# Feed-forward tile sums and splits moved from GpSimd to VectorE, with separated rings, four banks for the first pair and a pool shared by both products

## The chip, the cores and the metric

The kernel runs on one core of one Trainium2 chip. The metric is the device time of one execution in microseconds (us). Engines are named as in the profile: PE (TensorE, matmuls), DVE (VectorE), ACT (ScalarE), POOL (GpSimd), and SP, whose queue issues the DMAs.

## The reference

One decoder layer on a sequence of 1024 tokens of width 1024: an input projection, a state-space group and a sparse-attention group side by side, an output projection, and then the feed-forward part. The change touches the end of the output projection and the feed-forward part:

```
    mixed = jnp.concatenate([rms_norm(y_ssm, gn_ssm[i]), rms_norm(y_att, gn_attn[i])], axis=-1)
    x = x + g1 * (mixed @ w_out[i])
    h2 = rms_norm(x, norm2_g[i]) * (1.0 + sc2) + sh2
    ff = jnp.square(jax.nn.relu(h2 @ w_ff1[i])) @ w_ff2[i]
    x = x + g2 * ff
```

`w_ff1` is 1024 x 4096, `w_ff2` 4096 x 1024, all float32.

## The kernel before

Every float32 operand of a matmul is split in two float32r tiles: `hi`, a rounded copy made on ACT, and `lo`, the rest `x - hi`, a subtraction on DVE or POOL (`split`). A product of two such pairs is three matmuls, hi·hi, hi·lo and lo·hi (`mm3`, lines 89 to 91).

Both feed-forward products use a Strassen-Winograd scheme: 7 half-size products in place of 8, for which tiles must be added and subtracted first (operand sums) and results added and subtracted afterwards.

**Output projection (`outproj`).** Eight sequence tiles t = 0..7. `proj(t)` multiplies, and its result (`xn`, `x1`) is normalised; `modulate(t)` transposes it, scales it (`h`) and splits it into B: `b00`, `b10` for tiles 0 to 3, `b01` (called T1) and `b11` for tiles 4 to 7. T1 and `b11` are whole only after `modulate(7)`.

**First product (`ff_up`).** 16 steps i, each 256 columns of `w_ff1` (tile `w1r`, a ring of 2 buffers). Steps 0 and 1 are `plain` (8 products of 12 matmuls, no Winograd). Steps 2 to 15 are 7 products each: `prep` makes weight forms (`wsum` on POOL into ring `ws`, then `split` into ring `wf`), `step` multiplies. `tform(2..4)` make three more right-hand operands `t2`, `t3`, `t4` from the h tiles, by POOL subtractions (lines 1618 to 1622) and splits. `put` evacuates a bank with relu and square; `asum` (line 1660) makes four sums of the results on POOL, also in ring `ws`; `spill` sends the seven forms to DRAM (`a_d`). All of its tiles are in pool `ffu`, which is opened after `outproj` and closed at the end of `ff_up`.

**Second product (`ff_down`).** 4 groups of 7 product sets, q = 0..27. A set is 48 matmuls over four j; `loada` fetches four `a_d` tiles (`ax` or `ar`), `prep(q)` makes eight forms `fm` (16 tiles, ring of 36), with POOL sums `ts` in four of the seven sets; of the eight `lo` subtractions six are on DVE and two on POOL. `mms(q)` multiplies and adds the banks to `acc` on DVE (lines 1844, 1846). `w_ff2` comes in tiles `wr0`, `wr1`. `ada_g2` runs beside it: eight loads `awa` of `w_ada` into one buffer, each followed by a multiply-add on DVE. All its tiles are in pool `ffd`, opened after `ff_up`.

Each engine runs its own queue in order; the order is fixed when the program is built, from the order of the code and its priorities (`cur_priority`, smaller is earlier), and SP's queue of DMAs is in order too.

Of the kernel before, what the change touches and what calls it, by code (L numbers as in the profile page):

```python
# [45 lines left out]
MAXO = range(6)  # L46
LATER, TABN = 500, 1
# [12 lines left out]
class Kernel:  # L60
# [32 lines left out]
    def build(self):  # L93
        with ExitStack() as st:
# [1373 lines left out]
    def outproj(self, mxp):  # L1468
# [28 lines left out]
        def modulate(t):  # L1497
# [3 lines left out]
            for kk in range(2):  # L1501
# [12 lines left out]
                self.split(bh[:, :, tl], bl[:, :, tl], h, "s", "g")  # L1514
# [6 lines left out]
        def loadw1(c, A):  # L1521
            raw = op.tile([128, 1024], F32, name="w1r", tag="x1", bufs=2)
            raw = raw.rearrange("p (k n) -> p k n", k=KC)
            w1 = self.a["w_ff1"][0].rearrange("(p k) f -> p k f", k=8)
            D.dma_start(raw, w1[:, :, c * 128:(c + 1) * 128])
            for i in range(2):
                self.split(*A[i], raw[:, 4 * i:4 * i + 4], "s", "g")
# [13 lines left out]
        for i in range(2):  # L1541
            self.prod(self.ff_ps[i][:, 0], self.W1[i][0], self.B[0, 0], True)
# [20 lines left out]
    def ff_up(self):  # L1563
# [6 lines left out]
        fp, fclose = self.pool("ffu", side="right")  # L1570
# [4 lines left out]
        TT = {n: [fp.tile([128, 4, 512], F32R, name=f"t{n}{x}") for x in "hl"] for n in (2, 3, 4)}  # L1575
# [13 lines left out]
        def wsum(i, n):  # L1589
# [5 lines left out]
            G.tensor_tensor(SUM[i, n], x, y, op=op)  # L1595
# [14 lines left out]
        def tform(n):  # L1610
            for t in range(4):
                tl = slice(128 * t, 128 * t + 128)
                x = self.t2[t]
                if n > 2:
                    x = ws()
                    b = [f(z[:, :, tl]) for z in (B11 if n == 3 else B21)]
                    if n == 3:
                        G.tensor_tensor(x, self.t2[t], b[0], op=OP.subtract)
                        G.tensor_tensor(x, x, b[1], op=OP.subtract)
                    else:  # L1620
                        G.tensor_tensor(x, b[0], self.t2[t], op=OP.subtract)
# [31 lines left out]
        flat = lambda t: t.rearrange("p k n -> p (k n)")  # L1653

        def asum(i, n):
# [4 lines left out]
            G.tensor_tensor(o, x, y, op=op)  # L1660
# [7 lines left out]
        def plain(i):  # L1668
# [9 lines left out]
            else:  # L1678
                for r in range(2):
                    W[i, r] = self.W1[r]  # L1680
            for r in range(2):
                if i:
                    self.prod(X[r][:, 0], W[i, r][0], B11, True)
                keep(i, r, X[r][:, 0])
            for r in range(2):
                self.prod(X[r][:, 0], W[i, r][1], B21, False)
                put(i, r, 0, X[r][:, 0], None)
            for r in range(2):
                self.prod(X[r][:, 1], W[i, r][0], T1, True)
                self.prod(X[r][:, 1], W[i, r][1], B22, False)  # L1690
                put(i, r, 1, X[r][:, 1], C.pop((i, "k", r)))
            for n in range(1, 5):
                asum(i, n)
# [50 lines left out]
        prep(2, 2)
        tform(3)
        prep(2, 3)
        prep(2, 4)
        prep(2, 5)
        tform(4)
        prep(2, 6)  # L1750
# [14 lines left out]
        fclose()  # L1765

    def ff_down(self):
# [10 lines left out]
        def loadw(g, r):  # L1778
            for j in range(4):
                RAW[g, j, r] = fp.tile([128, 1024], F32, name=f"wr{r}", bufs=4)  # L1780
                D.dma_start(RAW[g, j, r], w2[8 * g + 2 * j + r])

        def loada(q):
            g, n = SEQ[q]
            for j in range(4):
                t = fp.tile([128, 512], F32, name="ar", bufs=4) if q % 2 else \
                    self.sct(j, n="ax").rearrange("p k n -> p (k n)")
# [3 lines left out]
        def form(x, lo):  # L1791
            w = [fp.tile([128, 512], F32R, name="fm", bufs=36) for _ in range(2)]
            self.split(*w, x, "s", lo)
# [32 lines left out]
        def mms(q):  # L1826
            g, n = SEQ[q]
            for t in range(4):
# [18 lines left out]
                if end and n == 4:  # L1847
                    z = fp.tile([128, 512], F32, name="ar", bufs=4)
# [6 lines left out]

        loadw(0, 0)
# [4 lines left out]
        prep(1)  # L1861
        acc = fp.tile([128, NT, 1024], F32, name="acc")
# [39 lines left out]
```

## Time and profile before

| | |
|---|---|
| median of 3 runs | 1410.95 us (1409.34 to 1411.72) |
| profiled execution | 1409.21 us, span of its instructions 1407.4 us |
| mean granted TensorE clock | 0.932 of full |
| PE busy | 1222.2 us (87%) |
| DVE busy | 992.0 us (70%) |
| ACT busy | 614.3 us (44%) |
| POOL busy | 776.0 us (55%) |

Times in a trace are counted from the span's first instruction. The profiled execution has 1.8 us outside its span and is 1.7 us below the median of the runs.

### The profile page before, as it was taken

What the parts mean: (1) busy time and instruction counts of PE and PEld (TensorE: products, weight loads), DVE (VectorE), ACT (ScalarE), POOL (GpSimd) and SP (SyncE); (2) the same over time, 40 slices, a digit from 0 to 9 for tenths busy, and PEclk for the clock granted to TensorE, in tenths of its full rate; (3) what the DMA queues carried; (4) which work ended last, traced back from release to release, by engine and by line L of the source; (5) the groups of instructions that cost most, each with busy time, mean ns of one, the idle gap of its engine ahead of it and who ended that gap; (6) DMA issues with size and microseconds to landing.
All of it is one profiled execution on the core that took longest, in us unless ns stands there. A gap on an engine that the chain in (4) does not pass through costs nothing.

```text
span 1407.4 us, 18661 instructions
## 1 busy us (share of the span) xinstructions
PE 1222.2 (87%) x6414; PEld 1041.5 (74%) x6414; DVE 992.0 (70%) x1618; ACT 614.3 (44%) x1231; POOL 776.0 (55%) x626
## 2 busy tenths in 40 slices
PE   4978987808898999999695899999978879999997
PEld 4867887807788899887584777777756658888885
DVE  6599956997886653377724666566539867767887
ACT  6454543747777767433312333233315224433340
POOL 3162899833632636334319556556639356663965
PEclk9898999967999989999897999999999989999999
DMA  9411234251333742322321243434336733536263
GB/s 331 114 47 39 74 99 130 74 131 25 82 85 98 233 141 91 105 90 98 105 98 67 97 157 129 149 135 165 142 145 245 243 123 105 202 98 219 89 194 120
DMA packets 119328, 179.84 MB, mean 128 GB/s; under 512 B 28864, under 2 KB 63680, under 8 KB 119232
## 3 DMA queue, kind: packets, MB, share of 16 engines
q1 hardware_dynamic: 118160, 178.61, 38.9%
q8 instruction: 50, 0.82, 0.3%
q14 instruction: 46, 0.38, 0.1%
q10 hardware_dynamic: 1072, 0.03, 0.0%
HBM read 128.92 MB, written 48.50 MB: 126 GB/s over the span
## 4 chain that ended last, share of the span: by engine, by line
PE 41%; DVE 9%; POOL 8%; issue 7%; DMA 3%; ACT 2%; SPq 0%; POOLq 0%; DVEq 0%; ACTq 0%
PE pS L89 8%; PE pS L90 8%; PE pS L91 8%; DVE fm L469 4%; PE pg L89 4%; PE pg L90 4%; PE pg L91 3%; POOL ws L1660 3%; POOL ws L1595 3%; PE po L1271 2%; DMA awa<-w_ada 1%; PE pg L1255 1%; PE pg L266 1%; DVE acc L1820 1%; DVE acc L1846 1%
## 5 line engine op out<-in xcount | busy, mean ns | idle before, releaser
L89 PE MATMUL pS<-fm 128*128 128x512 f32 x256 | 102.8, 406 | 22.3 <-ACT fm L467 10.4
L90 PE MATMUL pS<-fm 128*128 128x512 f32 x256 | 102.8, 403 | 3.6 <-DVE fm L469 3.5
L91 PE MATMUL pS<-fm 128*128 128x512 f32 x256 | 102.2, 400 | 0.0
L1660 POOL TENSOR_TENSOR ws<-c,c 128x512 f32<-128x512 f32 x15 | 19.6, 1309 | 145.8 <-DVE c L1649 145.8
L90 PE MATMUL pg<-wl,hh 128*128 128x256 f32 (+1 forms) x288 | 81.4, 284 | 13.1 <-POOL wl L469 13.1
L469 DVE TENSOR_TENSOR wf<-ws,wf 128x512 fp32r<-128x512 f32 x56 | 66.4, 1204 | 30.2 <-ACT wf L467 28.6
L89 PE MATMUL pg<-wh,hh 128*128 128x256 f32 (+1 forms) x288 | 80.9, 284 | 3.7 <-ACT wh L467 2.6
L467 ACT ACTIVATE fm<-ax 128x512 fp32r<-128x512 f32 x56 | 34.8, 621 | 107.6 <-PE pg L90 54.3
L1271 PE MATMUL po<-v,pt 128*128 128x64 f32 x576 | 77.6, 282 | 4.4 <-ACT pt L1258 3.4
L91 PE MATMUL pg<-wh,hl 128*128 128x256 f32 (+1 forms) x288 | 81.3, 283 | 0.0
L1271 PEld LDWEIGHTS po<-v,pt 128*128 128x128 f32 x576 | 76.1, 204 | 6.6 <-ACT pt L1258 3.8
L90 PE MATMUL pg<-fm 128*128 128x512 f32 x192 | 75.4, 393 | 2.9 <-DVE fm L469 2.9
L89 PEld LDWEIGHTS pS<-fm 128*128 128x128 f32 x256 | 49.7, 195 | 35.9 <-ACT fm L467 10.9
L557 DVE SCALAR_TENSOR_TENSOR sc<-r,wsgn,sc 128x384 f32<-128x384 f32 (+5 forms) x42 | 56.2, 1350 | 28.2 <-ACT r L553 27.1
L89 PE MATMUL pg<-fm 128*128 128x512 f32 x192 | 70.9, 391 | 5.5 <-DVE acc L1846 3.9
L469 DVE TENSOR_TENSOR fm<-wr,fm 128x512 fp32r<-128x512 f32 x64 | 66.4, 1049 | 13.2 <-ACT fm L467 13.2
L91 PE MATMUL pg<-fm 128*128 128x512 f32 x192 | 74.0, 390 | 0.0
L467 ACT ACTIVATE fm<-ar 128x512 fp32r<-128x512 f32 x56 | 34.7, 620 | 83.9 <-PE pS L90 62.3
L467 ACT ACTIVATE wf<-ws 128x512 fp32r<-128x512 f32 x56 | 35.3, 632 | 78.2 <-POOL ws L1595 77.9
L469 POOL TENSOR_TENSOR fm<-ax,fm 128x512 fp32r<-128x512 f32 x28 | 44.8, 1605 | 39.9 <-ACT fm L467 39.9
L469 POOL TENSOR_TENSOR fm<-ar,fm 128x512 fp32r<-128x512 f32 x28 | 44.7, 1601 | 38.7 <-ACT fm L467 37.9
L90 PEld LDWEIGHTS pg<-wl,hh 128*128 128x128 f32 x288 | 54.9, 191 | 14.1 <-POOL wl L469 13.5
(588 smaller groups left out, 4306.4 us busy)
## 6 DMA issues: line engine op xcount, KB each, us to landing
awa<-w_ada SPq DMA_DIRECT2D x32, 512.0 KB, 4.5
a_d<-ws SPq DMA_DIRECT2D x64, 256.0 KB, 2.0
wr<-w_ff SPq DMA_DIRECT2D x32, 512.0 KB, 5.4
w1r<-w_ff SPq DMA_DIRECT2D x15, 1024.0 KB, 5.3
ax<-a_d SPq DMA_DIRECT2D x56, 256.0 KB, 2.9
ar<-a_d SPq DMA_DIRECT2D x56, 256.0 KB, 2.9
a_d<-c SPq DMA_DIRECT2D x45, 256.0 KB, 2.0
x<-x SPq DMA_DIRECT2D x16, 512.0 KB, 5.2
```

The source lines that it names most:

```text
L89: T.matmul(out, lh, rh, start=start, stop=False, **kw)
L90: T.matmul(out, lh, rl, start=False, stop=False, **kw)
L91: self.pe = T.matmul(out, ll, rh, start=False, stop=stop, **kw).ins
L266: nc.tensor.matmul(ps[:, k:k + 1], acc.rearrange("p (q k) -> p k q", k=8)[:, k, :], self.ones[:, 0:1], start=True, stop=True)
L467: nc.scalar.activation(hi, x, AF.Copy)
L469: e.tensor_tensor(lo, x, f(hi), op=OP.subtract)
L557: V.scalar_tensor_tensor(sc, rv, self.wsgn[:, qt, h:h + 1], sc, op0=OP.mult, op1=OP.add)
L1255: T.transpose(ps[:, o:o + 128], P[n][h][:, (k0 + i) * 128:(k0 + i + 1) * 128], self.ident)
L1271: T.matmul(po[:, o:o + HD], pt[:, (2 * i + h) * 128:(2 * i + h + 1) * 128], self.v[:, k0 + i, kv * HD:(kv + 1) * HD], start=(o == 0 and k0 ...
L1595: G.tensor_tensor(SUM[i, n], x, y, op=op)
L1660: G.tensor_tensor(o, x, y, op=op)
L1820: e.tensor_tensor(d, d, self.g2[:, 512 * c:512 * c + 512], op=OP.mult)
```

## The change

All sums and all `lo` subtractions of the feed-forward part are made on DVE. The pool of `ff_up` is opened before `ff_up` and closed after `ff_down` (`ffp`: rings `w1r`, `wf`, `ws`, `c0`); `t2` to `t4` are in a pool of their own (`fft`). Steps 0 and 1 put the products with `b00` and `b10` into separate banks, so that four products of step 0 are written into four banks inside `outproj`. In `ff_down` the tiles `wr0`, `ar` and twelve of the forms (`fw`) take buffers of the rings `w1r`, `ws` and `wf` of `ffp`, the ring `fm` shrinks from 36 to 24, and the loads and forms of its first two sets get an earlier priority. The weight forms of `plain` and `tform(2)`, `tform(3)` stand ahead of step 0, `prep(i + 1, j)` stands ahead of `step(i, n)`, and `ada_g2` starts at set 8 of the code in place of set 3.

```diff
+EARLY = 500
...
+            self.ffp, ffp_close = self.pool("ffp", side="right")
             self.ff_up()
             w1_close()
             h2p_close()
             self.ff_down()
+            ffp_close()
...
-                self.split(bh[:, :, tl], bl[:, :, tl], h, "s", "g")
+                self.split(bh[:, :, tl], bl[:, :, tl], h, "s", "v")
...
-        for i in range(2):
-            self.prod(self.ff_ps[i][:, 0], self.W1[i][0], self.B[0, 0], True)
+        for j in range(2):
+            for i in range(2):
+                self.prod(self.ff_ps[i][:, j], self.W1[i][j], self.B[j, 0], True)
         modulate(NT - 1)
...
-        fp, fclose = self.pool("ffu", side="right")
+        fp = self.ffp
+        tp, tclose = self.pool("fft", side="right")
...
-            G.tensor_tensor(SUM[i, n], x, y, op=op)
+            V.tensor_tensor(SUM[i, n], x, y, op=op)
...
-                        G.tensor_tensor(x, self.t2[t], b[0], op=OP.subtract)
-                        G.tensor_tensor(x, x, b[1], op=OP.subtract)
+                        V.tensor_tensor(x, self.t2[t], b[0], op=OP.subtract)
+                        V.tensor_tensor(x, x, b[1], op=OP.subtract)
...
-            G.tensor_tensor(o, x, y, op=op)
+            V.tensor_tensor(o, x, y, op=op)
             spill(i, n + 2, o)
...
+        def plain(i, X):
+            for c, B in enumerate((B11, B21)):
+                for r in range(2):
+                    if i:
+                        self.prod(X[r][:, c], W[i, r][c], B, True)
+                    if c == 0:
+                        keep(i, r, X[r][:, 0])
+                    else:
+                        put(i, r, 0, X[r][:, 1], C.pop((i, "k", r)))
             for r in range(2):
...
+                self.prod(X[r][:, 0], W[i, r][0], T1, False)
+                self.prod(X[r][:, 0], W[i, r][1], B22, False)
+                put(i, r, 1, X[r][:, 0], None)
...
+        X0 = plain_forms(0)
+        X1 = plain_forms(1)
+        tform(2)
+        tform(3)
+        plain(0, X0)
...
+                prep(i + 1, j)
                 step(i, n)
-                prep(i + 1, j)
...
+                elif j % 2 == 0:
+                    two = self.ffp.tile([128, 2, 1024], F32, name="wr0", tag="w1r", bufs=2)
...
+        def form(q, j, x):
+            w = []
+            for _ in range(2):
+                if q % 2 == 0 and j < 3:
+                    t = self.ffp.tile([128, 4, 128], F32R, name="fw", tag="wf", bufs=12).rearrange("p k n -> p (k n)")
+                else:
+                    t = fp.tile([128, 512], F32R, name="fm", bufs=24)
+                w.append(t)
+            self.split(*w, x, "s", "v")
             return w
...
-                F[q, j] = form(AR.pop((q, j)), "g" if j % 2 else "v"), form(x, "v")
+                F[q, j] = form(q, j, AR.pop((q, j))), form(q, j, x)
...
+        self.tc.cur_priority -= EARLY
         loadw(0, 0)
         loada(0)
         prep(0)
         loada(1)
         loadw(0, 1)
         prep(1)
+        self.tc.cur_priority += EARLY
...
-            if q >= 3:
+            if q >= 8:
                 next(ada, None)
```

The changed code also moves instructions on the queues. The first place is DVE's queue at the end of `outproj`, from the evacuation of the last tile's projection to its normalisation (`xn`, `x` are the last tile's, `h_7603` and `h_7615` belong to tile 6). Before:

```order
L1508 TENSOR_TENSOR h_7603<-pg,s_95 128x512
L1487 TENSOR_TENSOR xn<-pS,g_6227 128x1024
L1508 TENSOR_TENSOR h_7615<-pg,s_95 128x512
L1509 TENSOR_TENSOR h_7603<-h_7603,b_96 128x512
L1488 TENSOR_TENSOR x_7536<-xn,x_7536 128x1024
L1509 TENSOR_TENSOR h_7615<-h_7615,b_96 128x512
L1512 TENSOR_TENSOR h_7603<-h_7603,b00h 128x512
L84 TENSOR_SCALAR rs_v_7594<-oss_7591 128x1
```

And now:

```order
L1511 TENSOR_TENSOR h_7603<-pg,s_95 128x512
L1490 TENSOR_TENSOR xn<-pS,g_6227 128x1024
L1511 TENSOR_TENSOR h_7615<-pg,s_95 128x512
L1512 TENSOR_TENSOR h_7603<-h_7603,b_96 128x512
L472 TENSOR_TENSOR wf<-w1r,wf 128x512
L1491 TENSOR_TENSOR x_7536<-xn,x_7536 128x1024
L472 TENSOR_TENSOR wf<-w1r,wf 128x512
L1512 TENSOR_TENSOR h_7615<-h_7615,b_96 128x512
L472 TENSOR_TENSOR wf<-w1r,wf 128x512
L1515 TENSOR_TENSOR h_7603<-h_7603,b00h 128x512
L472 TENSOR_TENSOR wf<-w1r,wf 128x512
L85 TENSOR_SCALAR rs_v_7594<-oss_7591 128x1
```

Four weight forms of step 1 (`wf`) now stand inside the last tile's chain.

The second place is POOL's queue of before between steps 1 and 2: the four `asum` of step 1, then weight sums of step 2 (line 1595) and the sums of `tform(3)` behind them:

```order
L1660 TENSOR_TENSOR ws<-c_7851,c_7867 128x512
L1660 TENSOR_TENSOR ws<-ws,c_7851 128x512
L1660 TENSOR_TENSOR ws<-c_7851 128x512
L1660 TENSOR_TENSOR ws<-c_7867,ws 128x512
L1595 TENSOR_TENSOR ws<-w1r 128x512
L1595 TENSOR_TENSOR ws<-ws,w1r 128x512
L1618 TENSOR_TENSOR ws<-sx_7394,b00h 128x512
L1618 TENSOR_TENSOR ws<-sx_7524,b00h 128x512
L1618 TENSOR_TENSOR ws<-sx_7620,b00h 128x512
L1618 TENSOR_TENSOR ws<-t2x,b00h 128x512
L1595 TENSOR_TENSOR ws<-w1r 128x512
L1619 TENSOR_TENSOR ws<-ws,b00l 128x512 x4
```

On DVE's queue of the changed kernel the sums and splits of `tform` stand between the two evacuations (line 1658 from `pS`) of step 0, ahead of both `asum` groups:

```order
L1627 TENSOR_TENSOR sx_7524<-sx_7524,b10l 128x512
L472 TENSOR_TENSOR w1a_7970<-w1r,w1a_7969 128x512
L1627 TENSOR_TENSOR sx_7620<-sx_7620,b10l 128x512
L1658 SCALAR_TENSOR_TENSOR c_7769<-pS,c_7769 128x512
L1627 TENSOR_TENSOR t2x<-t2x,b10l 128x512
L472 TENSOR_TENSOR t4l<-sx_7394,t4h 128x4x128
L472 TENSOR_TENSOR w1x_8022<-w1r,w1x_8021 128x512
L472 TENSOR_TENSOR t4l<-sx_7524,t4h 128x4x128
L472 TENSOR_TENSOR t4l<-sx_7620,t4h 128x4x128
L472 TENSOR_TENSOR w1x_8024<-w1r,w1x_8023 128x512
L1658 SCALAR_TENSOR_TENSOR c_7773<-pS,c_7773 128x512
```

The third place is the boundary between the two products. On SP's queue the first `w_ff2` tiles of before come after the last spills:

```order
L1640 DMA a_d_7681<-c1x 128x512
L1640 DMA a_d_7681<-ws 128x512 x4
L1781 DMA wr_10158<-w_ff 128x1024
L1781 DMA wr_10160<-w_ff 128x1024
L1781 DMA wr_10162<-w_ff 128x1024
L1781 DMA wr_10164<-w_ff 128x1024
```

Now the first pair (`wr_10158`) stands well ahead, and the second pair and `wr1` among the spills of step 15:

```order
L1800 DMA wr_10158<-w_ff 128x1024 x2
L1649 DMA a_d_7708<-c_9824 128x512
...
L1649 DMA a_d_7708<-c0x 128x512
L1800 DMA wr_10161<-w_ff 128x1024 x2
L1649 DMA a_d_7708<-c1x 128x512
L1649 DMA a_d_7708<-ws 128x512 x2
L1800 DMA wr_10212<-w_ff 128x1024
```

On DVE's queue at that boundary the changed kernel has, behind the last `asum` of step 14, sums of set 1 (`ts`) ahead of the first forms of set 0 (`fw`, `fm`), and sums of set 4 (line 1834) and the first multiply-add of `ada_g2` ahead of the forms of set 1:

```order
L1830 TENSOR_TENSOR ts<-wr_10161 128x512
L472 TENSOR_TENSOR fw<-ax_10164,fw 128x512
L472 TENSOR_TENSOR fm<-wr_10161,fm 128x512
L472 TENSOR_TENSOR fw<-wr_10158,fw 128x512
...
L1834 TENSOR_TENSOR wr_10161<-wr_10216,wr_10161 128x512
L1834 TENSOR_TENSOR wr_10161<-wr_10218,wr_10161 128x512
L1407 TENSOR_SCALAR aacc<-awa,silc 128x1024
L472 TENSOR_TENSOR fm<-ar,fm 128x512
L472 TENSOR_TENSOR fm<-ts,fm 128x512
```

In the code `ada_g2` starts later, on the queues its first load and multiply-add still stand at the boundary.

## Rows read from the trace of the kernel before

**Rows 1.** Busy time by stretch of the feed-forward part (columns in the first line)

```profile
core 0: us, PE busy (x) PEld busy (x) DVE busy (x) ACT busy (x) POOL busy (x), PEclk, DMA share, GB/s
680.00:697.00 17.00, 6.32 (x33) 4.95 (x32) 14.01 (x18) 4.46 (x9) 5.22 (x4) 0.84 0.48 155
...
740.00:792.00 52.00, 32.77 (x111) 24.72 (x110) 26.94 (x24) 14.38 (x24) 42.63 (x30) 0.77 0.17 61
792.00:1042.00 250.00, 241.91 (x1047) 195.66 (x1045) 151.72 (x171) 78.32 (x133) 139.45 (x98) 1.00 0.40 143
1042.00:1159.00 117.00, 86.90 (x344) 65.89 (x343) 90.33 (x90) 36.81 (x67) 72.80 (x46) 0.91 0.58 207
1159.00:1300.00 141.00, 141.00 (x616) 117.20 (x615) 104.06 (x124) 54.30 (x102) 77.89 (x51) 0.99 0.46 153
1300.00:1407.00 107.00, 97.78 (x418) 78.80 (x416) 92.36 (x98) 30.39 (x57) 77.30 (x49) 0.97 0.42 135
...
1111.00:1124.00 13.00, 11.39 (x51) 9.11 (x50) 11.68 (x18) 3.13 (x6) 1.29 (x1) 1.00 0.90 309
```

**Rows 2.** Waits of PE from 680 to 1160 us, longest in total

```profile
engine line waited for: us in total, times, longest us
PE pS L89 <- ACT kp L1665: 12.1, 1, 12.1
PE pg L89 <- ACT wf L467: 11.2, 7, 3.1
PE pS L89 <- ACT fm L467: 10.4, 1, 10.4
```

**Rows 3.** PE's timeline, the end of `outproj` (start, duration, instruction, idle before)

```profile
696.61 0.79 PE L89 MATMUL pS<-b10h,w1a 128*128 128x512 f32 x1 [5.62 <-ACT ws L1665]
697.21 0.63 PE L90 MATMUL pS<-b10l,w1a 128*128 128x512 f32 x1
...
701.04 0.63 PE L90 MATMUL pS<-b10l,w1a 128*128 128x512 f32 x1
...
704.58 0.39 PE L89 MATMUL pS<-b01h,w1a 128*128 128x512 f32 x1
```

**Rows 4.** POOL's timeline, the last tile's `lo` of T1

```profile
697.23 1.28 POOL L469 TENSOR_TENSOR b01l<-h,b01h 128x512 fp32r<-128x512 f32 x1
```

**Rows 5.** POOL's timeline between steps 1 and 2

```profile
739.57 1.30 POOL L1660 TENSOR_TENSOR ws<-c,c 128x512 f32<-128x512 f32 x1 [16.70 <-DVE c L1649]
...
747.22 4.64 POOL L1618 TENSOR_TENSOR ws<-sx,b00h 128x512 f32<-128x512 f32 x3
...
777.73 1.71 POOL L1595 TENSOR_TENSOR ws<-w1r 128x512 f32<-128x512 f32 x1
```

**Rows 6.** PE's timeline, first product with `b00` of step 4

```profile
795.15 0.39 PE L89 MATMUL pS<-b00h,w1a 128*128 128x512 f32 x1
...
797.65 0.40 PE L91 MATMUL pS<-b00h,w1a 128*128 128x512 f32 x1
```

**Rows 7.** PE's timeline, one of six like waits in the loop, and the last matmul of `ff_up`

```profile
853.49 0.50 PE L89 MATMUL pg<-b11h,wf 128*128 128x512 f32 x1 [1.41 <-ACT wf L467]
...
1045.50 0.39 PE L91 MATMUL pS<-t4h,wf 128*128 128x512 f32 x1
```

**Rows 8.** DVE by form from 792 to 1042 us (busy, mean ns of one, idle before)

```profile
L469 DVE TENSOR_TENSOR wf<-ws,wf 128x512 fp32r<-128x512 f32 x49 | 58.7, 1217 | 13.0 <-ACT wf L467 11.6
L1645 DVE TENSOR_TENSOR c<-pS,kp 128x512 f32<-128x512 f32 x24 | 16.4, 683 | 12.1 <-PE pS L91 12.1
```

**Rows 9.** DVE by form from 1111 to 1124 us, where POOL is nearly idle

```profile
L469 DVE TENSOR_TENSOR fm<-wr,fm 128x512 fp32r<-128x512 f32 x6 | 4.0, 677 | 0.0
```

**Rows 10.** DVE's timeline, three instructions back to back

```profile
1042.67 0.68 DVE L1645 TENSOR_TENSOR c0x<-pg,ws 128x512 f32<-128x512 f32 x1
1043.27 0.68 DVE L1649 SCALAR_TENSOR_TENSOR c1x<-c1x 128x512 f32<-128x512 f32 x1
1043.87 0.69 DVE L1649 SCALAR_TENSOR_TENSOR c0x<-c0x 128x512 f32<-128x512 f32 x1
```

**Rows 11.** SP's timeline, the first `w_ff2` loads

```profile
1051.80 1.88 SPq L1781 DMA_DIRECT2D wr<-w_ff x4
```

**Rows 12.** DVE by form from 1042 to 1159 us, at the boundary

```profile
L469 DVE TENSOR_TENSOR fm<-wr,fm 128x512 fp32r<-128x512 f32 x20 | 22.1, 1126 | 8.5 <-ACT fm L467 8.5
...
L1402 DVE SCALAR_TENSOR_TENSOR aacc<-awa,silc,aacc 128x1024 f32<-128x1024 f32 x7 | 11.7, 1673 | 11.8 <-DMA awa<-w_ada 11.8
```

**Rows 13.** DMA issues of the whole page (count, size, median us to landing)

```profile
wr<-w_ff SPq DMA_DIRECT2D x32, 512.0 KB, 5.4
w1r<-w_ff SPq DMA_DIRECT2D x15, 1024.0 KB, 5.3
```

**Rows 14.** PE's timeline, waits at the boundary and the program's last one

```profile
1056.33 1.22 PE L89 MATMUL pS<-fm 128*128 128x512 f32 x2 [10.44 <-ACT fm L467]
...
1399.70 0.50 PE L89 MATMUL pS<-fm 128*128 128x512 f32 x1 [1.38 <-DVE ar L1849]
```

More of the change, by code (lines that the diff above doesn't have):

```diff
@@ L1574, in ff_up @@
         self.a_d = [self.dram.tile([4, 7, 128, 512], F32, name=f"a_d{g}") for g in range(NP2 // 4)]
-        TT = {n: [fp.tile([128, 4, 512], F32R, name=f"t{n}{x}") for x in "hl"] for n in (2, 3, 4)}
+        TT = {n: [tp.tile([128, 4, 512], F32R, name=f"t{n}{x}") for x in "hl"] for n in (2, 3, 4)}
         B11, T1, B21, B22 = (self.B[q] for q in ((0, 0), (0, 1), (1, 0), (1, 1)))
@@ L1680, in plain @@
                     W[i, r] = self.W1[r]
-            for r in range(2):
[L1682 to L1693, printed above, removed]
+            return X
+        def plain(i, X):
[7 more added lines that the diff above has]
+                        put(i, r, 0, X[r][:, 1], C.pop((i, "k", r)))
+            for r in range(2):
+                self.prod(X[r][:, 0], W[i, r][0], T1, False)
+                self.prod(X[r][:, 0], W[i, r][1], B22, False)
+                put(i, r, 1, X[r][:, 0], None)
         def step(i, n):
@@ L1736, in ff_up @@
         self.W1 = {r: self.W1[r] for r in range(2)}
-        plain(0)
-        plain(1)
+        X0 = plain_forms(0)
[3 more added lines that the diff above has]
+        plain(0, X0)
+        for n in range(1, 5):
+            asum(0, n)
+        plain(1, X1)
+        for n in range(1, 5):
+            asum(1, n)
         del self.W1[0], self.W1[1]
-        tform(2)
         prep(2, 0)
         prep(2, 1)
+        prep(2, 2)
+        tform(4)
         load(3)
[L1744 to L1750, printed above, removed]
+        for j in range(3, 7):
+            prep(2, j)
         for i in range(2, NP2 - 2):
             for j, (n, _, _) in enumerate(ORDER):
+                prep(i + 1, j)
                 step(i, n)
-                prep(i + 1, j)
             if i + 2 < NP2:
@@ L1764, in ff_up @@
                 prep(LAST, j + 2)
-        fclose()
+        tclose()
     def ff_down(self):
@@ L1779, in loadw @@
             for j in range(4):
-                RAW[g, j, r] = fp.tile([128, 1024], F32, name=f"wr{r}", bufs=4)
-                D.dma_start(RAW[g, j, r], w2[8 * g + 2 * j + r])
+                if r:
+                    t = fp.tile([128, 1024], F32, name="wr1", bufs=4)
+                elif j % 2 == 0:
+                    two = self.ffp.tile([128, 2, 1024], F32, name="wr0", tag="w1r", bufs=2)
+                if not r:
+                    t = two[:, j % 2]
+                RAW[g, j, r] = t
+                D.dma_start(t, w2[8 * g + 2 * j + r])
         def loada(q):
@@ L1785, in loada @@
             for j in range(4):
[L1786 to L1787 removed]
+                t = self.ffp.tile([128, 4, 128], F32, name="ar", tag="ws", bufs=6) if q % 2 else self.sct(j, n="ax")
+                t = t.rearrange("p k n -> p (k n)")
                 D.dma_start(t, self.a_d[g][j, AIX[n]])
                 AR[q, j] = t
[L1791 to L1793 removed]
+        def form(q, j, x):
[7 more added lines that the diff above has]
+            self.split(*w, x, "s", "v")
             return w
@@ L1847, in mms @@
                 if end and n == 4:
-                    z = fp.tile([128, 512], F32, name="ar", bufs=4)
+                    z = fp.tile([128, 512], F32, name="z", tag="ts", bufs=4)
                     V.tensor_tensor(z, o, g2(), op=OP.mult)
@@ L1878, in ff_down @@
                         t += 0 if n == 6 else 4
-                        X[t] = fp.tile([128, 1024], F32, name="x1", tag=f"wr{t // 4}", bufs=4)
+                        if t >= 4:
+                            X[t] = fp.tile([128, 1024], F32, name="x1", tag="wr1", bufs=4)
+                        elif t % 2 == 0:
+                            two = self.ffp.tile([128, 2, 1024], F32, name="x1w", tag="w1r", bufs=2)
+                            X[t], X[t + 1] = two[:, 0], two[:, 1]
                         D.dma_start(X[t], self.x1_d[t * 128:(t + 1) * 128, :])
```

36 lines of the change are left out of this document (19 added, 17 removed).

## The prediction

> **What bounds the kernel now.** I read the busy time by stretch first [rows 1], because the share of the whole span (PE 87%) hides where PE stands still. From 1159 to 1300 us PE is busy throughout. It is idle for 10.7 of 17 us at the end of `outproj`, 19.2 of 52 us between steps 1 and 2, 8.1 of 250 us in the loop, 30.1 of 117 us at the boundary of the two products and 9.2 of 107 us at the end: 77 us in all. So the change can gain at most these 77 us and what the low clock behind them costs.
>
> The waits of PE [rows 2] name the last releaser: ACT copies. ACT itself is not late. At 740 us POOL is busy for 42.63 of 52 us [rows 1], and its timeline is one row of sums from 739.57 to 779.4 us [rows 5]; the ACT copies wait for those sums. In the loop POOL has the same place: PE waits 1.41 us at 853.49 [rows 7] for a copy of the fourth weight sum, which stands behind three `asum`. At the boundary PE waits 10.44 us [rows 14] for forms whose `w_ff2` tiles SP issues only at 1051.80 [rows 11], behind the last spills of POOL's sums, and DVE then stays busy for 90 of 117 us.
>
> The price of a matmul is (797.65 - 795.15) / 11 = 0.227 us [rows 6], a product of 12 is 2.73 us, a set of 48 10.9 us. Behind a long wait, at the granted clock's lower level, it is (701.04 - 697.21) / 9 = 0.426 us [rows 3]; some eleven matmuls run so, 11 x 0.199 = 2.2 us.
>
> **The change part by part.** *The price of a moved sum.* A DVE operation on two SBUF operands takes 1217 ns in the loop [rows 8] and 1126 ns at the boundary [rows 12], but 677 ns where POOL is busy for 1.29 of 13 us [rows 9], and an operation with one operand in PSUM 683 ns even beside POOL [rows 8]. Three in a row start 0.60 us apart [rows 10]. I take 0.60 us for all of DVE's operations once POOL is silent. The bounds are 0.60 and 1.2 us. I am near the lower one since the row that lacks POOL has it. The 276 instructions that leave POOL's queue then cost DVE 166 us; the 49 of [rows 8] alone give back 49 x 0.62 = 30 us.
> The Trainium skill, page SBUF — State Buffer, section Who interferes with whom, says that a DVE instruction with two SBUF inputs and a GpSimd instruction that reads SBUF exclude each other for the whole instruction. By that, each such operation should be back at 0.60 us, and a DVE operation beside a POOL sum of 1.3 us [rows 5] could take 1.9; the sum below would be the same.
>
> *End of `outproj`.* T1's first product starts at 704.58 us [rows 3]. Its last operand is ready at 697.23 + 1.28 = 698.5 [rows 4], but two products with `b10` run first, because their banks wait for a copy into a `ws` buffer that comes late [rows 3]. Now four products run ahead of T1's operand, in PE's idle time. Is the operand itself earlier? The last tile's chain loses POOL's subtraction and DVE's contention (two operations of some 1.7 us become 0.7), but four `wf` subtractions, two sums of `tform(3)` and two more `lo` stand in it, 8 x 0.60 = 4.8 us. I count this even: 698.5, then 2.2 us of slow matmuls. Gain 704.6 - 698.5 - 2.2 = 4 us, between 0 (a `w1r` load of 5.3 us [rows 13], on which the first `wf` waits, is late by 4) and 6.
>
> *Steps 0 to 3.* From 704.58 to 795.15 us [rows 3, 6] PE runs 23 products, 62.8 us of work in 90.6: 27.8 us lost. After the change the sums are 0.60 us each, spread before steps 0 and 1, and the forms of step 2 need eight DVE operations behind step 1's last bank, 5 us, while two products (5.5 us) run. Left over: step 1 takes over step 0's banks, and the two evacuations stand in DVE's queue behind some 23 and 7 operations, 13.8 and 4.2 us, where PE has 13.0 and 2.7 us of work: 0.8 + 1.5 us, with the dependent operations some 3; one wait of 1 us for step 2's first weight form; 2 us for what I do not see. Lost 6; gain 22, between 14 (half of the loss stays) and 25.
>
> *The loop.* From 795.15 to 1045.73 us [rows 6, 7] PE runs 87 products, 237.5 us of work in 250.6: 13.1 us lost, 8.1 of them in six waits of 1.3 to 1.4 us. DVE now has 22 operations per step, 13.2 to 14.5 us of the 19.1 us that PE needs, and the four weight sums stand a step ahead. I expect the six waits gone, one of 1.2 us at the last step (its last form stands behind an evacuation) and the wider spacing kept: lost 5, gain 8, between 0 and 12.
>
> *The boundary.* Of the idle 30.1 us [rows 1] 0.6 belong to the loop; with two slow stretches (4 us) 33.5 are lost. Now the first `wr0` pair is loaded during the last steps, but the second takes the buffer of step 15's weights and is issued where its last form is done, 5.4 us before it lands [rows 13]; and DVE's queue has 14 operations from there to the first usable pair of set 0, 8.4 us, of which the last product covers about 2. So PE waits some 7 us (10.44 before), then 2.2 us at the lower clock. Behind that, DVE makes the forms of sets 0 to 6: 56 subtractions, 16 sums, 24 evacuations at 0.60 and 8 multiply-adds at 1.2 us are 67 us, while PE needs 65.5 for the six sets ahead of the last form, with a start 7 us later. That just fits, and I add 5 us for operations that stand in the wrong order. Lost 14; gain 19. Bounds: 9 lost if all fits, 26 if the 11.8 us in which DVE waits for `awa` [rows 12] stay: gain 7 to 25.
>
> *Sets 7 to 27.* The rings hold one set ahead, as the ring of 36 did. DVE per set: 8 + 16/7 two-operand operations and 4 evacuations, 14.3 x 0.60 = 8.6 us of PE's 10.9. No gain up to 1300 us, where PE is full [rows 1]; of the 9.2 us idle later some 5 are the last store. There I take 3 us of gain, between 0 and 6.
>
> *Sum.* 4 + 22 + 8 + 19 + 3 = 56 us. The profiled execution has 1409.2 us, so 1353; the median of the runs is 1.7 us higher: 1355. All the lower bounds together give 21 us, 1390; all the upper ones 74, 1337.
>
> **The rivals.** *DVE becomes the bound* (slower). In the last 107 us DVE is already busy for 92 [rows 1]. If its two-operand operations kept 1.05 us beside silent POOL, a step of the loop would have 18 of them and 4 others, 21.3 us against 19.1, and a set 10.3 x 1.05 + 2.4 = 13.2 us against 10.9: 13 x 2.2 + 28 x 2.3 = 93 us more, 1355 + 93 = 1448. It decides from 0.83 us per operation, where a set takes DVE as long as PE, and the kernel is slower than before from about 0.95. For it: the mean of today. Against it: 677 ns without POOL [rows 9], 0.60 apart [rows 10]. The Trainium skill, page Perfetto Trace Analysis, section Optimizing Scalar/DVE Operations, would take work off a saturated DVE, to GpSimd too, though it adds that the shared port may spoil this. By its first half this change goes the wrong way; no row here bears that half out. I give it 5%.
>
> *DVE's order takes the place of POOL's.* POOL's sums were late, but did not hold up evacuations and forms; in one queue they do. If the boundary keeps 26 us lost, steps 0 to 3 keep 14 and the loop keeps its waits, the gain is 4 + 14 + 0 + 7 + 3 = 28 us: 1383; with the loop's waits gone, 1375. For it: sums of sets 1 and 4 and the `awa` multiply-add stand ahead of forms that PE waits for. 20%.
>
> *The waits are not POOL's.* If the products waited for the loads (`w1r` 5.3 us [rows 13]), only the four banks and the earlier `wr0` would tell, 5 to 10 us: 1403. Against it: POOL's unbroken row [rows 5]. 3%, and 2% that nothing changes.
>
> **How the numbers follow.** The forecast, 1338 to 1368, has 63%; DVE's order (1368 to 1388) 20%; the loads 3%; no change 2%; the bound on DVE 5%; a gain above 73 us 7%. The last one follows if PE is full from T1 on. The range 1338 to 1385 holds the forecast and all but the end of the second case, some 81%. A change of 0.2%, 3 us, is about what a measurement of this kernel can tell from none. Faster: 63 + 20 + 3 + 7 = 93%; same 2%; slower 5%.
>
> **What would show it.** Right: DVE's two-operand operations at 0.7 us in the loop and in `ff_down`; PE busy for at least 45 of 52 us after the start of step 1; no wait of 1.3 us every second step; the first matmul of `ff_down` some 7 us behind the last of `ff_up`; `awa` no longer among DVE's long waits. Wrong: mean durations above 0.83 us with POOL silent; PE's waits now named after DVE in the loop; T1's first product later than 702 us; a boundary that still loses more than 25 us.

## The result and the profile after

| | before | changed |
|---|---|---|
| median of 4 runs each | 1410.15 us (1409.34 to 1411.72) | 1360.64 us (1356.31 to 1362.38) |
| ratio, with its 95% interval | 1 | 0.9643 (0.9618 to 0.9668) |
| profiled execution | 1409.21 us | 1360.31 us |
| PE, DVE, POOL busy | 1222.2, 992.0, 776.0 us | 1216.1, 1017.4, 364.7 us |
| DVE instructions | 1618 | 1894 |

The change takes 49.5 us off. DVE got 276 instructions more and is busy for only 25 us more: at 0.60 us each they are 166 us, so some 140 us came back from the instructions that it had already.

Three stretches carry all that follows. *Projections*: from the first matmul with `woh` to T1's first product. *First product*: from there to the last matmul of `ff_up`. *Second product*: from there to the end of the span.

| us in the profiled execution | projections | first product | second product | sum |
|---|---|---|---|---|
| before | 130.8 | 340.9 | 361.9 | 833.6 |
| changed | 123.9 | 310.2 | 349.7 | 783.8 |

The busy time by stretch of the changed kernel, with the columns of [rows 1]:

```profile
680.00:697.00 17.00, 8.68 (x42) 6.83 (x40) 16.52 (x27) 5.31 (x10) 1.46 (x1) 0.88 0.26 95
740.00:792.00 52.00, 51.22 (x221) 40.85 (x220) 39.57 (x64) 20.90 (x35) 0.00 (x0) 1.00 0.40 143
792.00:1005.00 213.00, 213.00 (x927) 173.74 (x925) 148.47 (x232) 68.37 (x114) 0.00 (x0) 1.00 0.41 150
1005.00:1122.00 117.00, 104.56 (x425) 82.41 (x425) 100.68 (x157) 43.83 (x81) 0.00 (x0) 0.94 0.64 214
1122.00:1263.00 141.00, 137.01 (x593) 111.54 (x592) 108.28 (x177) 53.53 (x99) 0.64 (x1) 1.00 0.50 159
1263.00:1358.50 95.50, 86.18 (x358) 68.83 (x357) 76.64 (x102) 25.31 (x46) 31.75 (x20) 0.96 0.37 124
```

PE, idle for 19.2 of 52 us from 740 us before, is now busy for 51.22 of them, and for all of the loop. What idle time is left lies at both ends of the projections' last tile and in the second product. PE's timeline at the places of [rows 3, 6, 7, 14], and at two new waits late in the second product:

```profile
698.54 0.80 PE L90 MATMUL pS<-b01h,w1a 128*128 128x512 f32 x1 [7.98 <-DVE c L1654]
...
770.36 0.40 PE L90 MATMUL pS<-b00h,w1a 128*128 128x512 f32 x1
...
1008.76 0.39 PE L92 MATMUL pS<-t4h,wf 128*128 128x512 f32 x1
1013.40 1.00 PE L90 MATMUL pS<-fw 128*128 128x512 f32 x2 [4.25 <-ACT fw L470]
...
1025.74 2.08 PE L90 MATMUL pg<-fm 128*128 128x512 f32 x4 [5.04 <-ACT fm L470]
...
1262.20 0.50 PE L90 MATMUL pS<-fw 128*128 128x512 f32 x1 [2.85 <-DVE acc L1871]
...
1344.80 0.79 PE L90 MATMUL pS<-fm 128*128 128x512 f32 x1 [2.99 <-DVE z L1874]
```

The first wait of the second product has shrunk from 10.44 to 4.25 us, but a second one of 5.04 us follows it. DVE by form, the loop's main form as in [rows 8], and the boundary's multiply-adds as in [rows 12]:

```profile
L472 DVE TENSOR_TENSOR wf<-ws,wf 128x512 fp32r<-128x512 f32 x41 | 28.0, 685 | 2.5 <-ACT wf L470 2.5
...
L1405 DVE SCALAR_TENSOR_TENSOR aacc<-awa,silc,aacc 128x1024 f32<-128x1024 f32 x7 | 9.0, 1280 | 2.0 <-DMA awa<-w_ada 2.0
```

685 ns in place of 1217, and 1280 in place of 1673. The changed kernel still has POOL sums near its end, so one stretch of it shows what they do. DVE's timeline there, and POOL's:

```profile
1331.27 1.78 DVE L472 TENSOR_TENSOR fm<-ar,fm 128x512 fp32r<-128x512 f32 x1
1332.97 1.78 DVE L472 TENSOR_TENSOR fm<-ts,fm 128x512 fp32r<-128x512 f32 x1
1334.67 1.77 DVE L472 TENSOR_TENSOR fm<-ar,fm 128x512 fp32r<-128x512 f32 x1
1336.37 0.68 DVE L1871 TENSOR_TENSOR acc<-pS,acc 128x512 f32<-128x512 f32 x1
...
1338.68 0.67 DVE L472 TENSOR_TENSOR fm<-ar,fm 128x512 fp32r<-128x512 f32 x1
```

```profile
1332.46 3.43 POOL L1846 TENSOR_TENSOR acc<-acc,x1w 128x512 f32<-128x512 f32 x2
1335.86 1.74 POOL L1846 TENSOR_TENSOR acc<-acc,x 128x512 f32<-128x512 f32 x1
```

The same form takes 1.78 us while POOL adds, and 0.67 us a microsecond after POOL has stopped; the evacuation with one operand in PSUM takes 0.68 us beside POOL too.

### The profile page after: what moved, and what is told of

It is laid out like the page before. It is cut to its first block, busy times and chain, and to the rows that moved or that the text cites. A ratio compares the mean times of both kernels' runs of the same rounds, so it can differ in the third digit from the quotient of the medians.

```text
span 1358.5 us, 18554 instructions
## 1 busy us (share of the span) xinstructions
PE 1216.1 (90%) x6414; PEld 1038.1 (76%) x6414; DVE 1017.4 (75%) x1894; ACT 616.7 (45%) x1231; POOL 364.7 (27%) x350
## 4 chain that ended last, share of the span: by engine, by line
PE 51%; DVE 12%; DMA 4%; ACT 2%; issue 2%; POOL 2%; SPq 1%; DVEq 0%; ACTq 0%; POOLq 0%
PE pS L90 10%; PE pS L91 10%; PE pS L92 10%; PE pg L90 5%; PE pg L91 5%; PE pg L92 5%; DMA awa<-w_ada 2%; PE po L1274 2%; DVE fm L472 2%; PE pg L269 1%; PE pg L1258 1%; DVE acc L1871 1%; DVE acc L1845 1%; DVE fw L472 1%; POOL wol L472 1%
## 5 line engine op out<-in xcount | busy, mean ns | idle before, releaser
L90 PE MATMUL pS<-fm 128*128 128x512 f32 x160 | 62.2, 400 | 4.7 <-DVE z L1874 4.4
L91 PE MATMUL pS<-fm 128*128 128x512 f32 x160 | 63.1, 397 | 0.3 <-DVE fm L472 0.3
L92 PE MATMUL pS<-fm 128*128 128x512 f32 x160 | 62.9, 395 | 0.0
L1245 DVE CUSTOM_DVE_ANT_0 P<-pS,sc,rq 128x384 f32<-128x384 f32 (+5 forms) x48 | 43.9, 941 | 20.9 <-PE pS L1241 12.8
L90 PEld LDWEIGHTS pg<-wh,hh 128*128 128x128 f32 x288 | 54.3, 190 | 5.0 <-ACT wh L470 2.8
L556 ACT ACTIVATE r<-pS,wabs 128x384 f32<-128x384 f32 (+5 forms) x48 | 40.6, 848 | 36.4 <-PE pS L552 27.7
L92 PEld LDWEIGHTS pg<-wh,hl 128*128 128x128 f32 x288 | 54.9, 191 | 0.4
L1261 ACT ACTIVATE pt<-pg 128x512 f32<-128x512 f32 (+1 forms) x80 | 42.2, 547 | 22.2 <-PE pg L1258 21.8
L1258 PE MATMUL pg<-ident,P 128*128 128x128 f32 x288 | 49.2, 292 | 3.0 <-DVE zl L1340 1.3
L1247 ACT ACTIVATE P<-P,mx 128x128 f32<-128x128 f32 (+7 forms) x64 | 49.1, 769 | 5.7 <-DVE mx L1245 5.5
L90 PE MATMUL pS<-woh,mh 128*128 128x512 f32 x128 | 51.2, 400 | 0.0
L92 PE MATMUL pS<-woh,ml 128*128 128x512 f32 x128 | 50.9, 398 | 0.0
```

Source lines behind the costliest of these rows:

```text
L90: T.matmul(out, lh, rh, start=start, stop=False, **kw)
L91: T.matmul(out, lh, rl, start=False, stop=False, **kw)
L92: self.pe = T.matmul(out, ll, rh, start=False, stop=stop, **kw).ins
L556: S.activation(rv, ps[:, :, :n], AF.Relu, scale=self.wabs[:, qt, h:h + 1])
L1245: V.tensor_tensor_reduce(pv, ps[:, :nj, :m], bv, scale=self.rq[:, qt, h:h + 1], scalar=-NEG, op0=OP.add, op1=OP.min, accum_out=mx)
L1247: S.activation(p[:, :w], p[:, :w], AF.Exp, scale=-1.0, bias=mx, accum_out=LS[qt][:, h:h + 1])
```

## The experiments

The theory: POOL's sums were late and held DVE up, and both made PE's waits, so the move to DVE brings the gain. The rival: the banks, the rings, the held pool and the new order bring it.

**The engine alone, and everything but the engine.** `b_vec` is the kernel before with this edit, at all the places of the diff that change an engine:

```diff
-            G.tensor_tensor(SUM[i, n], x, y, op=op)
+            V.tensor_tensor(SUM[i, n], x, y, op=op)
```

> The kernel before, with only the engine changed: every feed-forward sum and lo subtraction on VectorE, nothing else. Theory (POOL's one late queue and its interference with DVE make PE's waits): the loop's 8 us, most of the loss of steps 0 to 3 (some 15 of 28) and a third of the boundary's come without any other edit, about 1380 us, DVE's two-operand operations at 0.6 to 0.7 us. Rival (the four banks, the held pool and the earlier loads bring it): 1400 to 1412 us, PE's waits as before.

`a_pool` is the changed kernel with the reverse edit.

> The changed kernel with the sums and the alternate lo splits back on GpSimd, rings, banks, held pool, order of the code and early loads kept. Theory: most of the gain is lost again, 1385 to 1400 us, DVE's two-operand operations back at 1.1 to 1.2 us, PE's waits in the loop and between steps 1 and 2 back. Rival (structure brings it): 1358 to 1368 us.

| us | median | ratio to before | projections | first | second |
|---|---|---|---|---|---|
| `b_vec` | 1357.24 | 0.9631 (0.9611 to 0.9651) | 124.8 | 315.4 | 342.8 |
| `a_pool` | 1396.56 | 0.9900 (0.9880 to 0.9921) | 129.5 | 323.7 | 365.0 |

The engine alone brings 52 us, no less than the whole change and 23 more than I expected of it; everything else alone brings 13, and on top of the engine nothing. One and the same wait can go by either, so the two gains don't add. PE's six waits in the loop are gone in `b_vec`, where the weight sums still stand behind the step, and in `a_pool`, where they stand a step ahead but run on POOL: either cure is enough, so my expectation that `a_pool` would bring them back was wrong; DVE's `wf<-ws` is back at 1069 ns there, as expected. By stretch, the new arrangement gains 17.2 us in the first product while the sums are on POOL (340.9 to 323.7), 5.2 on DVE (315.4 to 310.2), and it costs 3.1 and 6.9 us in the second product. PE's waits of `b_vec` from 680 to 1122 us:

```profile
PE pS L89 <- ACT fm L467: 8.7, 1, 8.7
PE pS L89 <- ACT kp L1665: 6.5, 1, 6.5
PE pS L89 <- ACT ws L1665: 4.9, 1, 4.9
PE pS L89 <- DVE acc L1844: 4.9, 1, 4.9
```

The waits of [rows 2] are still there by name, but shorter: 12.1 for `kp` is 6.5, the seven for `wf` are gone.

**POOL beside DVE, with nothing waiting for it.** `a_beside`:

```diff
+        self.dz = fp.tile([128, 512], F32, name="dz")
+        G.memset(self.dz, 0.0)
...
+        def idle():
+            G.tensor_tensor(self.dz, self.dz, self.dz, op=OP.mult)
...
             V.tensor_tensor(SUM[i, n], x, y, op=op)
+            idle()
...
             V.tensor_tensor(o, x, y, op=op)
+            idle()
             spill(i, n + 2, o)
```

> The changed kernel, with one more multiplication of 128x512 on GpSimd for every weight sum and result sum of the first product, 120 of them on a tile that nobody else reads; nothing waits for them, and the order of DVE, PE and SP stays as it is. They run back to back from about 697 us, some 160 to 200 us. If POOL beside DVE costs by itself: DVE's two-operand operations of that stretch take 1.2 us or more, a step 18 x 1.2 + 4 x 0.6 = 24 us of DVE against 19.1 of PE, and 200 us x (1 - 19.1 / 24) = 40 us are lost: about 1400. If only the place of the sums in POOL's queue mattered: 1359 to 1364 us, operations at 0.68 us.

Measured: 1422.19 us (ratio 1.0096, 1.0058 to 1.0133), 1% slower than before and on the side of the first theory. Busy time by stretch and DVE by form from 700 to 900 us:

```profile
700.00:900.00 200.00, 153.84 (x600) 121.03 (x601) 172.05 (x170) 52.27 (x89) 138.49 (x105) 0.87 0.26 93
900.00:1060.00 160.00, 160.00 (x697) 130.54 (x696) 111.99 (x176) 51.44 (x86) 0.00 (x0) 1.00 0.40 145
```

```profile
L472 DVE TENSOR_TENSOR wf<-ws,wf 128x512 fp32r<-128x512 f32 x24 | 25.1, 1054 | 0.0
...
L1660 DVE TENSOR_TENSOR c<-pS,kp 128x512 f32<-128x512 f32 x10 | 6.9, 686 | 6.7 <-PE pS L92 6.7
```

POOL's added row ends at 846.6 us. PE's 46 us of idle time in the first window all lie before that, and there is none behind it. So the interference is enough by itself to make such waits, without any late sum. Its share in the 49.5 us is not shown by this: POOL is busy for 138 of the 147 us from 700 to 847 here, but for only 139 of 250 in the loop of before. It cost 61.6 us, not 40: the two-operand operations took 1054 ns, less than the 1.2 us that I had put in, but I had costed DVE's rate alone. Where DVE's operations hang on one another PE waited for 17.1 us ahead of T1 and 16.8 us at the first take-over of a bank, against 7.98 and 1.1 in the changed kernel. What POOL's late queue costs apart from interference stays open in the main, since its sums can't be run without it. Two places show that its order counted too. In the loop of `a_pool` DVE's forms still take 1069 ns and the six waits are gone: slow forms alone don't make them there, the late place of the sums was needed too. And between steps 1 and 2 of the kernel before, POOL stood idle for 16.70 us ahead of its row of sums [rows 5]: its queue had step 1's result sums first, which waited for DVE, and step 2's weight sums behind them. No run puts these weight sums ahead while they stay on POOL.

**The early priority.** `a_noearly` has `EARLY = 0`.

> The changed kernel with EARLY = 0, so the loads and forms of the first two sets of the second product keep the priority of their place in the code. Theory (the held pool makes the early loads possible, the priority only moves a load of w_ada by some places on SP's queue): 1358 to 1366 us. Rival (the priority is what brings the boundary's gain): 1367 us or more, with the first wr loads behind 1012 us.

1360.10 us (0.9638, 0.9614 to 0.9662): no difference, as the theory had it. The second product takes 350.9 us in place of 349.7.

**The second product as before.** `a_old_down` keeps the first product as changed and takes `ff_down` of `b_vec`:

```diff
             self.ff_up()
+            ffp_close()
...
-                if q % 2 == 0 and j < 3:
-                    t = self.ffp.tile([128, 4, 128], F32R, name="fw", tag="wf", bufs=12)...
+            w = [fp.tile([128, 512], F32R, name="fm", bufs=36) for _ in range(2)]
...
```

> The changed kernel's first product with the second product of before on VectorE (pool of the first one closed at its end, rings of their own for wr0, ar and fm with 36 tiles, no early priority, ada_g2 from set 3). Theory (the changed arrangement of the first product is worth 6.3 us, that of the second one costs 6.9, each in its own stretch): 333.5 us from the last projection matmul to the last of ff_up, 342.8 from there to the end, 1351 to 1354 us. Rival (the two hang together, the shorter second product comes from how the first one of before ends): 1357 to 1361 us.

1352.37 us (0.9608, 0.9578 to 0.9637), stretches 310.2 and 341.9: the two halves are independent, and the changed arrangement of the second product (held pool, shared rings and the later start of `ada_g2` in the code, which no run separates) costs some 8 us. It starts the second product earlier (4.6 us behind the last matmul of `ff_up` against 7.9), but its first set takes 11.6 us more than 48 matmuls of 0.227 us, that of `a_old_down` 1.9.

**The second wait at the boundary.** ACT's timeline of the changed kernel shows what PE's second wait hangs on:

```profile
1024.54 0.63 ACT L470 ACTIVATE fm<-ar 128x512 fp32r<-128x512 f32 x1 [9.11 <-DMA ar<-a_d]
```

SP issues these loads behind six `wr` and one `awa`. `a_ar` gives three of these tiles other buffers:

```diff
-                t = self.ffp.tile([128, 4, 128], F32, name="ar", tag="ws", bufs=6) if q % 2 else ...
+                t = self.sct(4 + j, n="ay") if q == 1 and j < 3 else self.ffp.tile(...
```

> The changed kernel with three of the four ar tiles of set 1 in buffers of the keep ring, free before the last step ends, in place of ws buffers, which come free when the last spills have landed. Theory (PE's second wait at the boundary, 5.05 us, is for ar loads issued late and queued behind 3 MB of wr and awa): wait and slow matmuls go, 5 to 7 us, 1353 to 1356 us. Rival (the same transfers share the DMA engines anyway, and the fourth tile comes from the last step): 1358 to 1363 us.

1359.41 us (0.9651, 0.9615 to 0.9688), second product 351.9: no gain. PE's waits from 1005 to 1095 us say why:

```profile
PE pS L90 <- ACT fw L470: 6.2, 2, 5.9
PE pS L90 <- DVE acc L1871: 3.8, 1, 3.8
PE pS L90 <- DVE acc L1869: 2.1, 1, 2.1
PE pg L90 <- ACT fm L470: 0.3, 1, 0.3
```

The wait of 5.04 us for `ar` is gone, but the first wait is 5.9 us in place of 4.25, and 5.9 us of waits for evacuations on DVE have come in sets 3 to 5. The load was the last to arrive, but DVE sets the pace behind it; the next runs test that.

**Is the boundary DVE's?** Two ways to take 10 us off DVE there, both on `a_old_down`. Busy time of `a_old_down` behind its first matmul:

```profile
1012.00:1056.00 44.00, 42.88 (x181) 35.35 (x182) 43.49 (x71) 22.82 (x41) 0.00 (x0) 0.94 0.79 281
```

`od_ada` moves the eight multiply-adds of `ada_g2` behind set 10's loads:

```diff
-            nc.sync.dma_start(wa, wada[:, k, 5 * 1024:])
+            with self.tc.issue_after(self.ld):
+                nc.sync.dma_start(wa, wada[:, k, 5 * 1024:])
...
-                D.dma_start(t, self.a_d[g][j, AIX[n]])
+                self.ld = D.dma_start(t, self.a_d[g][j, AIX[n]]).ins
```

> The faster mix of the last runs (first product as changed, second as before on VectorE), with the loads awa of ada_g2 queued behind those of set 10, so its eight multiply-adds leave the boundary. Theory (the boundary is DVE's: it is busy without a gap from 1012 to 1070 us, 9.7 us of that are these multiply-adds, and one waits 2.54 us for its load with forms queued behind it): PE's wait of 4.91 us at set 6 and the slow matmuls behind it, 6.8 us in all, go: 1345 to 1348 us; the first wait of 7.5 us, for wr, stays. Rival (forms and evacuations alone fill DVE there): 1351 to 1354 us.

`od_copy` moves the copies of the first group to ACT:

```diff
-                    V.tensor_copy(d, o)
+                    S.activation(d, o, AF.Copy)
```

> The same mix, with the 16 copies of banks into acc in the first group on ScalarE in place of VectorE (9.6 us less for DVE, 9.6 more for ACT, which is busy for half of that stretch). Theory (DVE is the bound behind the boundary): PE's 6.8 us at set 6 shrink to 0 to 4: 1346 to 1350 us. Rival (the copies wait in ACT's queue behind hi copies, and PE waits for its banks): 1353 us or more.

`od_copy`: 1345.38 us (0.9548, 0.9529 to 0.9567), second product 334.8; set 6 loses nothing, in place of 6.8 us. In the matching 44 us behind its first matmul DVE is busy for 38.63:

```profile
1016.00:1060.00 44.00, 43.17 (x182) 35.53 (x183) 38.63 (x60) 29.06 (x53) 0.00 (x0) 0.94 0.83 285
```

`od_ada`: 1353.72 us (0.9605, 0.9585 to 0.9625), second product 342.9, within the rival's range and no gain on `a_old_down`. It too takes the wait at set 6 away (1.1 us left of 4.9), but PE waits later, in set 13. The second row here is DVE's, from the stretch before that wait:

```profile
1171.84 0.80 PE L91 MATMUL pg<-fm 128*128 128x512 f32 x1 [4.04 <-DVE fm L472]
1153.08 1.29 DVE L1406 SCALAR_TENSOR_TENSOR aacc<-awa,silc,aacc 128x1024 f32<-128x1024 f32 x1 [2.90 <-DMA awa<-w_ada]
```

So DVE is the bound at the boundary, as the theory had it: both edits that take work off it there end the wait at set 6. But my new place for the multiply-adds was bad. One of them kept DVE idle for 2.90 us until its load had landed, with forms queued behind it. From 1153.1 to 1175.4 us DVE was then busy without a gap, and the form that PE waits for at 1171.84 us stands in that row.

**Sums left on POOL at the end.** `a_tail_v`:

```diff
-            G.tensor_tensor(d, d, X[t][:, 512 * c:512 * c + 512], op=OP.add)
+            V.tensor_tensor(d, d, X[t][:, 512 * c:512 * c + 512], op=OP.add)
...
-                        gate(t, 0, G)
+                        gate(t, 0, V)
```

> The changed kernel with its last sums on GpSimd (acc + x1, and four multiplications by g2) on VectorE too. Theory (beside each POOL sum DVE's two-operand operations take 1.78 us in place of 0.68, so evacuations are late): PE's wait of 2.99 us near the end and the slow matmuls behind it go, 4 to 5 us, 1355 to 1357 us. Rival (20 more operations of 0.6 us fill DVE, which then has the last word): 1360 to 1366 us.

1353.96 us (0.9617, 0.9590 to 0.9645); the second product takes 345.6 us, 4.1 less, and the wait of 2.99 us is 0.95. These 4 us are as expected. The median lies 6.7 us below that of the changed kernel and 1 us below the expected range; 2.5 us of that are, in the profiled executions, ahead of the projections, where nothing was changed.

**More products ahead of T1.** `a_gbanks` gives step 1 four banks of the other ring:

```diff
+                Y = [self.bank() for _ in range(4)]
+                X = [(Y[r], Y[r + 2]) for r in range(2)]
...
```

> The changed kernel with four banks of the other ring for step 1, so that three of its products (8.2 us) stand ahead of T1's first product in PE's queue, in the 8 us in which PE is idle there, and step 1 no longer takes over step 0's banks. Theory (PE is full from T1 to the end of ff_up, so every product moved ahead of T1 is worth its time): 8 us, less 1 to 2 us by which T1's product may start later, and 2 us of the lower clock less: 1350 to 1354 us. Rival (the evacuations of step 1 fill DVE's queue and PE waits for the forms of step 2): 1358 to 1363 us.

1358.17 us (0.9635, 0.9605 to 0.9664), a miss: it lies in the rival's range, and the difference to the changed kernel is within the spread of the runs. From the first projection to the end of `ff_up` 430.8 us in place of 434.1: 3.3 us of the expected 8. PE's timeline and DVE's (cut to the sums) show where the rest went:

```profile
737.09 0.80 PE L90 MATMUL pg<-b01h,wf 128*128 128x512 f32 x1 [5.33 <-ACT wf L470]
```

```profile
733.15 0.69 DVE L1667 TENSOR_TENSOR ws<-c,c 128x512 f32<-128x512 f32 x1
...
735.69 0.69 DVE L1600 TENSOR_TENSOR ws<-w1r 128x512 f32<-128x512 f32 x1
```

The first weight sum of step 2, whose operands had been loaded long before, stands behind the result sums of step 1. `od_gb2` has the same banks on `a_old_down`, and the order of these sums changed:

```diff
-        for n in range(1, 5):
-            asum(1, n)
...
         prep(2, 2)
+        for n in range(1, 5):
+            asum(1, n)
```

> The same mix, with step 1 in four banks of the other ring (three of its products ahead of T1's first one) and the first weight sums of step 2 ahead of the result sums of step 1. Theory (the four banks of step 1 were worth 8 us, of which 5.33 were given back in a wait for weight sums that stood behind the result sums for a ws buffer): from the last projection matmul to the last of ff_up 333.5 - 3.3 - 5.3 = 325 us, 1343 to 1346 us. Rival (the evacuations of step 1 come too late whatever the sums' order): 1348 to 1353 us.

1343.05 us (0.9530, 0.9513 to 0.9547); 423.3 us to the end of `ff_up`, against 434.1 in `a_old_down`: 10.8 us, and no wait of a microsecond between T1 and the last step.

**Together.** `best` is `od_gb2` with the edits of `od_copy` and `a_tail_v`.

> The parts that the runs before speak for, together: first product as changed with step 1 in four banks of the other ring and step 2's first weight sums ahead, second product as before on VectorE, its 16 copies of the first group on ScalarE, and the last sums on VectorE instead of GpSimd. Theory (the gains lie in separate stretches and add): 1343.1 - 7 (set 6) - 4 (the end) = 1332 us, 1329 to 1336. Rival (a gain is given back in a later stretch, as with ada_g2): 1338 to 1345 us.

1326.35 us (1324.28 to 1328.34, 5 runs), ratio 0.9389 (0.9370 to 0.9408): 86 us faster than before, and more than expected of it: beside `od_gb2` the second product fell from 342.8 to 329.8 us, 13 in place of 11, and T1 began 1.8 us earlier in its stretch (126.8 us against 128.6); why was not followed up. PE's waits from 680 us to the end, the four longest:

```profile
PE pS L90 <- ACT fm L470: 8.1, 1, 8.1
PE pg L1507 <- DVE xn L1497: 1.9, 1, 1.9
PE pS L90 <- DVE ar L1866: 1.7, 2, 1.4
PE pg L91 <- DVE fm L472: 1.4, 1, 1.4
```

More than half of what waits are left there, 8.1 of 14.7 us, is the first wait of the second product, where ACT waits 6.2 us for `wr`. The held pool of the changed kernel has 4.25 us there, but at the price shown above.

## Why the prediction was right

1355 us were forecast and 1360.64 measured. The mechanism held: without POOL's sums DVE's operations are short, and PE's waits between steps 1 and 2 and in the loop are gone. Its terms were mixed, and that some of them came out was luck.

- **Price of a moved sum.** 685 ns in the loop, 0.60 us apart: as taken from the row that lacked POOL. The Trainium skill, SBUF — State Buffer, section Who interferes with whom, has a DVE operation with two SBUF inputs and a GpSimd operation that reads SBUF exclude each other for the whole instruction; the trace agrees nearly, with 1.78 us beside POOL's sums, where the prediction worked out 1.9, and 0.68 us for an operation with a PSUM operand. The Trainium skill, Perfetto Trace Analysis, section Optimizing Scalar/DVE Operations, would consider work for GpSimd where DVE is full, with the shared port as its reserve; the runs bear the reserve out, since the sums on GpSimd cost 36 us (`a_pool`), and GpSimd work that nothing waits for 61.6 (`a_beside`).
- **End of `outproj`, 4 us.** T1's first product starts at 698.54 us, as worked out, and some ten matmuls behind it run slow. But the step "now four products run ahead of T1's operand" is not where most of it comes from: `b_vec`, without the four banks, shortens the projections by 6.0 us, the whole change by 6.9, and the banks with POOL's sums (`a_pool`) by 1.3. The product then waited for an evacuation of step 0 (line 1654), 1.3 us behind its operand.
- **Steps 0 to 3, 22 us.** From T1 to the first product of step 4 it took 71.82 us for 24 products, against 90.57 for 23: 90.57 - 71.82 + 2.73 = 21.5. Left over were 6.3 us, forecast 6; but 2.2 of them are the slow matmuls behind T1, which the prediction had counted in the term before.
- **The loop, 8 us.** 340.9 - 310.2 - 21.5 = 9.2. One wait of 0.88 us at the last step, forecast 1.2.
- **The boundary, 19 us.** From the last matmul of `ff_up` to set 7 it took 115.15 us before and 95.90 now: 19.3. The first wait was 4.25 us, not 7, and a second one of 5.04 us that I did not have made up for it. That the 19 came out is luck: from the last matmul of `ff_up` to set 7 PE lost some 38.7 us before, not 33.5, since beside 29.5 us of waits, matmuls at the lower clock cost 9.2 us and not the 4 that I put in, and now it loses 19.4, not 14. Both are short by some 5 us. `b_vec` takes 93.50 us there without any early load. That `awa` would no longer be among DVE's waits was wrong: 3.7 us of 11.8 stayed. That DVE's work "just fits" was wrong as well: `od_copy` shows it to be the bound.
- **Sets 7 to 27, 3 us of gain.** This step failed: they lost 7.1 us (241.70 to 248.77, from the first matmul of set 7 to the last of all). "The rings hold one set ahead, as the ring of 36 did" costed the shared rings at nothing; with rings of their own and the same engine (`a_old_down`) these sets take 243.98 us. At 1262.20 us an evacuation stood behind ten forms and sums in DVE's queue, which is the second rival, at a place that I had not looked at. And at the end the sums that stay on POOL cost 4.1 us (`a_tail_v`). With both out of the way, in `best`, these sets take 237.62 us: 4.1 less than before, about the 3 that were forecast.
- **What the sum could not say.** It gave each part a gain on top of the others. The runs show that the engine alone gives all of it, and that the changed arrangement takes back in the second product (6.9 us) what it brings in the first (5.2) and in the projections (0.9).

## What to carry to other kernels

Where operations of two engines slow each other, a moved operation is priced by what it frees in the instructions that stay, not by its own time: 276 more instructions cost DVE 25 us here. When a change has several cures for one wait, run each alone before the next is built on it; here one edit had the whole gain, and half of the rest was a loss. A load that arrives last is not the bound until it has been given for nothing: in `a_ar` the wait only changed its name, and the engine behind it was to be relieved.

## What was unexpected of the hardware

- Interference costs more than a rate: 120 POOL operations of 1.32 us on their own tile, 159 us of POOL time, made the kernel 61.6 us slower, though PE and DVE ran the same instructions in the same order.
- In the projections, operations with one tile as operand were also faster in the changed kernel: the `TENSOR_SCALAR` `mixs<-mixs` 128x512 485 ns in place of 877, `xn<-x` 128x1024 750 in place of 1180. It is the engine and not the arrangement: `b_vec`, which moves the sums alone, has 485 and 750 ns, and `a_pool`, which has everything but the move, 877 and 1182.
